# Streaming-encoder layer: projection weights split a block at a time ahead, and head pages prepared two score tiles ahead

## The chip, the cores and the metric

The kernel runs on one core of one Trainium2 chip. The metric is the device time of one execution in microseconds; less is better. It is given as the median of several runs.

A core has five engines that work side by side: TensorE (PE) multiplies matrices, VectorE (DVE), ScalarE (ACT) and GpSimd (POOL) work element by element, and SyncE (SP) issues the transfers (DMA). Each engine executes its own queue in order. An instruction that waits holds up all that stands behind it in the same queue.

## The reference, cut to what matters

One layer on a sequence of 1024 tokens of width 1024, in float32. The part that the change touches is the mixer:

```
h    = modulate(rmsnorm(x), shift, scale)
proj = h @ w_in                    # one input projection, its columns split:
  q_lat (256), kv_lat (128), k_rope (32)      -> latent attention, 8 heads
  ca_qkv (3 x 8 heads x 64)                   -> chunked attention, 8 heads
chunked: q, k normed per head; scores over a band of 9 chunks of 64 keys
         + a clipped relative bias; softmax; values
latent:  q, k, v from the normed latents by two up-projections; q, k normed,
         rotary on 32 of 96 dims; chunk-causal scores; softmax; values
x = x + gate * (concat(latent, chunked) @ w_out)
```

After it comes a gated MLP with a depthwise convolution, which the change does not touch.

## The kernel before, in words

**Numbers.** A float32 product is made of three matmuls on rounded parts: each operand is split into a high part (a copy, line 77, on ACT) and a low part (the difference, line 84, mostly on POOL), and `gemm3` (lines 150 to 157) multiplies high by high, high by low and low by high. So every block of weights has to be fetched, copied and subtracted before PE can use it.

**Fetching weights.** `load_w` (lines 175 to 196) takes a weight of the input projection in eight blocks of 128 rows. For each block it issues a DMA into a raw buffer (tag `wr`, 3 buffers), makes the high part on ACT and the low part on POOL (tag `ws`, 16 buffers). A block of up to 256 columns takes one `ws` buffer, a block of the 416-column weight `w_m` takes two, in two pieces each of its own raw buffer. For the second value weight a Square per block on ACT sums up the squares as well (line 192).

**Two kinds of work share the engines.** The first is attention: 32 units, first 16 of chunked attention, `(c, pair of heads p, half of the queries g, head o)`, then 16 of latent attention, `(m, group, head, half g)`. Each unit has four score tiles of 128 queries. A unit first needs its *pages*: `ca_pages` (713 to 732, for both heads of a pair at once) and `qk_page` (700 to 711) transpose the normed q and k on PE into one PSUM bank (tag `T`, a single buffer; the tiles are `q_ps`, `k_ps`, `mq_ps`, `mk_ps`) and split them on ACT, DVE and POOL. `Unit.scores` (742 to 834) multiplies into one of two score buffers (tag `S`), takes the minimum of the negated scores on DVE (`mc`, `mm`, lines 786 and 790), the exp on ACT (797), splits the probabilities into two halves of 16 bits on POOL and DVE (73 and 819) and transposes them by DMA (831). `Unit.values` (836 to 874) multiplies them by the values.

The second kind is called *fillers* (lines 931 and 932), in this order: `v0`, `qk1`, `qk2`, `v1`, `qk3` (the input projection, a pair of heads or two at a time), `m` (its latent columns, with transposes `lt_ps` of the normed latents into the bank `T`), `up0`, `up1` (the up-projections), `oca` (half of the output projection). Each is a generator; one step is six matmuls or so. A q/k or v projection has 32 steps: four output tiles of two rows of eight blocks, two blocks a step. `f_qk`, `f_v` and `f_m` call `load_w` for all eight blocks at their first step. In `f_qk` the ACT instructions of this call are queued behind `anchor["act"]`, the Square that was traced last in `qk_norm`.

**What sets the order.** The program is written once as a trace. The loop in lines 984 to 996 goes over the score tiles, prepares a unit just before its first tile (`need(u.need)`, `u.prep()`), traces its scores and, three tiles later, its values, and after each calls `pace` (968 to 975), which traces filler steps until their estimated cost makes up 1.9 times (chunked) or 0.5 times (latent) that of the piece of attention. `need` traces all steps of the fillers that a unit depends on. A scheduler then puts each engine's instructions into a queue: by their place in the trace, scores moved ahead by an offset of 400, probabilities and values by 200, and as inputs and buffers come free in its own estimate of time. On the chip the queues run as they were written. A filler's matmuls are also kept behind the score or value matmuls that were traced five pieces earlier (`trail`, `LAG`, lines 161 to 172), so that fillers cannot run far ahead of attention. A side stream `f_ada` on SP, DVE and PE computes further modulation vectors; `fill_step` (937 to 957) advances it with the fillers, and the rotary tables with `qk1`.

Behind these stages come the rest of the output projection and the MLP, lines 1004 onward.

Of the kernel before, what the change touches and what calls it, by code (L numbers as in the profile page):

```python
# [13 lines left out]
F32 = mybir.dt.float32  # L14
# [10 lines left out]
P = 128  # L25
# [3 lines left out]
ND = D // P  # L29
# [7 lines left out]
NM = QR + KVR + ROPE  # L37
# [27 lines left out]
def layer_kernel(ctx, tc, I, out):  # L65
# [49 lines left out]
    anchor = {}  # L115
# [56 lines left out]
            yield 3 * len(part) * max(107, w / 2.4 + 2.5)  # L172


    def load_w(name, src, ncol, he="a", ssw=None):
        tiles = []
        for k in range(ND):
            if ncol <= 256:
                w = hw.tile([P, 2, 256], F32R, name=f"{name}s{k}", tag="ws", bufs=16)
                hi, lo = w[:, 0, :ncol], w[:, 1, :ncol]  # L180
            else:
                wh = hw.tile([P, 512], F32R, name=f"{name}h{k}", tag="ws", bufs=16)
                wl = hw.tile([P, 512], F32R, name=f"{name}l{k}", tag="ws", bufs=16)
                hi, lo = wh[:, :ncol], wl[:, :ncol]
            for c0 in range(0, ncol, 256):
                c = slice(c0, min(c0 + 256, ncol))
                raw = hw.tile([P, 256], F32, name=f"{name}r{k}_{c0}", tag="wr", bufs=3)
                rw = raw[:, :c.stop - c0]
                anchor["sp"] = sp.dma_start(rw, src[:, k, c]).ins
                if ssw is not None:  # L190
                    junk = qtile(f"{name}j{k}")
                    act.activation(junk[:, :c.stop - c0], rw, AF.Square, accum_out=ssw[:, k:k + 1])
                hi_of(he, hi[:, c], rw)
                lo_of("p", lo[:, c], rw, hi[:, c])
            tiles.append((hi, lo))
        return tiles


    sp.dma_start(pos_i[:], I["pos"])
# [47 lines left out]
    wv0, wv0r = [], []  # L247
# [113 lines left out]

    qns, vts = {}, {}

    def f_qk(p):
        with tc.issue_after(anchor["act"]), tc.issue_after(r_last):
            w = load_w(f"wq{p}_", I["w_qk"][p], 256)
        for h in range(2):
            qns[p, h] = pgtile([P, 4, 256], F32, f"qn{p}_{h}")
        for t in range(0, NT, 2):
            pt = ps.tile([P, 512], F32, name=f"ipq{p}_{t}", tag="mm", bufs=2)  # L370
            yield from proj2(pt, t, w, 256)
            qk_norm(pt[:], f"{p}_{t}", qns[p, t // 4], t % 4)

    def f_v(pp):
        ssw = cst.tile([P, ND], F32, name=f"ssw{pp}") if pp else ssw0
        w = load_w(f"wv{pp}_", I["w_v"][pp], 256, ssw=ssw) if pp else wv0
        for t in range(0, NT, 2):
            h, j = divmod(t, 4)
            if t == 0:
                for i in range(2):  # L380
                    vts[2 * pp + i] = apg.tile([P, NT, 2, 2, 64], F16, name=f"v{2 * pp + i}", tag="v16", bufs=3)
            pt = ps.tile([P, 512], F32, name=f"ipv{pp}_{t}", tag="mm", bufs=2)
            yield from proj2(pt, t, w, 256)
            if t == 0:
                vscale["c", pp] = pow2_scale(f"c{pp}", ssw[:], hb[:], ND, 2.0 * D)
                sc = vscale["c", pp][0]
            for i in range(2):
                vt = vts[2 * pp + i][:, t:t + 2]
                src = pt[:].rearrange("p (t q a b) -> p t q a b", t=2, q=2, a=2)[:, :, i]
                act.activation(vt[:, :, :, 0, :], src, AF.Copy, scale=sc)  # L390
                dve.scalar_tensor_tensor(vt[:, :, :, 1, :], src, sc, vt[:, :, :, 0, :], op0=MUL, op1=SUB)
# [78 lines left out]
    def f_m():  # L470
        for _ in rope[0]:
            pass
        w = load_w("wm_", I["w_m"], NM)
        lat = {}
        for t in range(NT):
            h, j = divmod(t, 4)
            sl = slice(j * P, (j + 1) * P)
            pt = ps.tile([P, 512], F32, name=f"mp_{t}", tag="mm", bufs=2)
            yield from gemm3_f(pt[:, :NM], [(hT[k, h][:, 0, sl], hT[k, h][:, 1, sl]) + w[k] for k in range(ND)])
            raw = rtile(f"lat_{t}")  # L480
            act.activation(raw[:, :NM], pt[:, :NM], AF.Copy)
            sq = qtile(f"msq_{t}")
            ss = cst.tile([P, 2], F32, name=f"mss_{t}", tag="ss", bufs=4)
            r = cst.tile([P, 2], F32, name=f"mr_{t}", tag="rr", bufs=4)
            act.activation(sq[:, :QR], raw[:, :QR], AF.Square, accum_out=ss[:, 0:1])
            act.activation(sq[:, QR:QR + KVR], raw[:, QR:QR + KVR], AF.Square, accum_out=ss[:, 1:2])
            act.activation(sq[:, QR + KVR:NM], raw[:, QR + KVR:NM], AF.Square, accum_out=ssr[:, t:t + 1])
            pool.tensor_scalar(ss[:, 0:1], ss[:, 0:1], 1.0 / QR, EPS, op0=MUL, op1=ADD)
            rsqrt_mean(r[:], ss[:], KVR, cols=slice(1, 2))
            pool.tensor_scalar(raw[:, :QR], raw[:, :QR], r[:, 0:1], 1.0, op0=MUL, op1=MUL)  # L490
            pool.tensor_scalar(raw[:, QR:QR + KVR], raw[:, QR:QR + KVR], r[:, 1:2], 1.0, op0=MUL, op1=MUL)
            rope_apply(kr[:, t:t + 1, :], raw[:, QR + KVR:NM].unsqueeze(1), tabk, t, 1, raw[:, NM:NM + 64])
            lat[t] = raw
            if j == 3:
                for b in range(3):
                    ptt = ps.tile([P, 512], F32, name=f"lt_ps{h}_{b}", tag="T", bufs=TB)
                    for jj in range(4):
                        pe.transpose(ptt[:, jj * P:(jj + 1) * P], lat[4 * h + jj][:, b * P:(b + 1) * P], ident[:])
                    pg = pgtile([P, 2, 512], F32R, f"latT{h}_{b}")
                    gain = pk[:, C_GQL + b:C_GQL + b + 1]  # L500
                    act.activation(pg[:, 0], ptt[:], AF.Copy, scale=gain)
                    dve.scalar_tensor_tensor(pg[:, 1], ptt[:], gain, f32(pg[:, 0]), op0=MUL, op1=SUB)
                    latT[b, h] = pg
                    yield 436
# [410 lines left out]
    def mla_unit(gr, hh, g):  # L915
        o = hh % 2

        def prep():
            q = qk_page(lambda j: mq[gr, (4 * g + j) // 2][:, j % 2, hh, :], f"mq{gr}{hh}_{g}", QK, "Q", 2, None)
            k = qk_page(lambda j: mk[gr, (4 * g + j) // 2][:, j % 2, hh, :], f"mk{gr}{hh}_{g}", QK, "K", 3, gk_m[:QK])  # L920
            pages[gr, hh, g] = (q, k)
        u = Unit(f"m{gr}{hh}", 0, QK,
                 lambda: (pages[gr, hh, g][0], [pages[gr, hh, i][1] for i in range(g + 1)]),
                 lambda j: mv[gr, j // 2][:, j % 2, hh].rearrange("p a b -> p (a b)"),
                 g, False, None, o, oT_d[2 * gr + hh // 2], ("m", gr))
        u.prep = prep
        u.need = [f"up{gr}"] if g == 0 else ["up1"]
        u.needv = []
        return u
# [3 lines left out]
    done = set()  # L933
    side = [f_ada()]
    nside = [0]

    def fill_step():
        while fillers:
            key, gen = fillers[0]
            try:  # L940
                c = next(gen)
            except StopIteration:
                done.add(key)
                fillers.pop(0)
                continue
            if key == "qk1":
                if rope[0] is None:
                    rope[0] = rope_tables()
                with tc.issue_after(anchor["dve"]):
                    next(rope[0], None)  # L950
            if key not in ("v0", "up0", "up1", "oca"):
                nside[0] += c
                while nside[0] > 1700:
                    nside[0] -= 1700
                    next(side[0], None)
            return c
        return None
# [22 lines left out]
    first = [anchor["pe"]]  # L980
    units = [ca_unit(p, g, o) for p in range(4) for g in range(2) for o in range(2)]
    units += [mla_unit(gr, hh, g) for gr in range(2) for hh in range(4) for g in range(2)]
    tiles = [(u, i) for u in units for i in range(4 * u.g, 4 * u.g + 4)]
    for n in range(len(tiles) + DEPTH):
        if n < len(tiles):
            u, i = tiles[n]
            if i % 4 == 0:
                need(u.need)
                u.prep()
            pace(u.scores(i), R_CA if u.band else R_MLA)  # L990
        if n >= DEPTH:
            u, i = tiles[n - DEPTH]
            if i % 4 == 1:
                need(u.needv)
            if i % 2:
                pace(u.values(i), R_CA if u.band else R_MLA)
# [609 lines left out]
```

## Time and profile before

| | us |
|---|---|
| median of 3 runs | 1346.02 (1341.62 to 1346.54) |
| the profiled execution | 1345.89 |
| its span, first to last instruction | 1344.1 |
| PE busy | 1223.8 (91%) |
| DVE busy | 1096.2 (82%) |
| ACT busy | 622.7 (46%) |
| POOL busy | 578.1 (43%) |
| from the first score tile to the last value tile | about 86 to 627 |

In the profile's rows an instruction stands as `line engine operation out<-in`, by the names of the program's tiles with their numbers left out: `wq_s` and `wv_s` are split weights, `ipq`, `ipv` and `mp` the projections' results, `sc` and `sm` scores of chunked and latent attention, `pvc` and `pvm` values. `xN` is the count; then come the busy time in us and the mean duration of one in ns, and behind the second bar the time that the engine stood idle just before them and what ended it. In a timeline the start and the duration come first. In the views by stretch each engine has its busy time and count. A busy PE is not a PE at its peak: the granted clock says how fast it ran.

### The profile page before, as it was taken

To read this page: it belongs to the slowest core of one execution; us is meant where nothing else is said; L and a number is where in the kernel's file an instruction comes from. 1 tells how busy PE (TensorE), PEld (TensorE's weight loads), DVE (VectorE), ACT (ScalarE), POOL (GpSimd) and SP (SyncE) were. 2 spreads that over 40 slices of the span, in tenths; PEclk is the share of its full clock that TensorE was granted. 3 is DMA by queue.
4 is the path that set the end of the run, shared out by engine and by line. 5 is a ranking of instruction groups with operands and counts; after the bars stand their busy time and mean duration, and the time that the engine had idled before them with its cause. 6 is when DMAs were issued, how large, how long until landed. Compare 5 with 4: busy or idle time off the path is not lost.

```text
span 1344.1 us, 18696 instructions
## 1 busy us (share of the span) xinstructions
PE 1223.8 (91%) x6168; PEld 1003.8 (75%) x6168; DVE 1096.2 (82%) x1928; ACT 622.7 (46%) x1132; POOL 578.1 (43%) x610
## 2 busy tenths in 40 slices
PE   4899798998877798886998999999999998999998
PEld 3788587896655567765776888888888886888886
DVE  6978798864679987894989988988899997687667
ACT  4453546443555544563376444444434444433431
POOL 5464557565646763354634444444445431000000
PEclk9899798998787889996999999999999998999999
DMA  8415577854413477779911333333323326943441
GB/s 323 138 35 116 135 177 179 192 127 110 87 32 80 94 153 165 141 150 252 377 49 47 126 110 133 103 122 98 133 102 118 126 98 241 390 141 117 130 161 63
DMA packets 223689, 190.57 MB, mean 142 GB/s; under 512 B 148708, under 2 KB 166884, under 8 KB 223592
## 3 DMA queue, kind: packets, MB, share of 16 engines
q1 hardware_dynamic: 223592, 189.38, 49.1%
q8 instruction: 48, 0.79, 0.2%
q14 instruction: 49, 0.40, 0.1%
HBM read 117.24 MB, written 37.49 MB: 115 GB/s over the span
## 4 chain that ended last, share of the span: by engine, by line
PE 41%; DVE 10%; issue 3%; ACT 2%; DMA 1%; POOL 1%; SPq 0%; DVEq 0%; ACTq 0%; POOLq 0%
PE p L1082 7%; PE p L1084 7%; PE p L1083 7%; PE dnA_P L1417 2%; PE dnA_P L1419 2%; PE dnA_P L1418 2%; PE dnB_P L1419 1%; PE dnB_P L1418 1%; PE dnB_P L1417 1%; DVE u L1253 1%; DVE u L1254 1%; PE op L154 1%; PE dnA L1417 1%; PE dnA L1419 1%; PE dnA L1418 1%
## 5 line engine op out<-in xcount | busy, mean ns | idle before, releaser
L77 ACT ACTIVATE dnP<-dnr 128x1024 fp32r<-128x1024 f32 x73 | 77.5, 1064 | 117.5 <-PE dnA_P L1419 46.4
L1391 DVE TENSOR_TENSOR dnP<-dnr,dnP 128x1024 fp32r<-128x1024 f32 x72 | 87.9, 1223 | 52.6 <-ACT dnP L77 52.6
L73 POOL TENSOR_SCALAR hlm<-Pm,rim 128x512 f16<-128x512 f32 (+3 forms) x96 | 68.8, 726 | 83.5 <-DVE rim L800 22.3
L84 POOL TENSOR_TENSOR wf<-wu,wf 128x512 fp32r<-128x512 f32 x22 | 38.8, 1762 | 116.3 <-ACT wf L77 116.3
L1253 DVE SCALAR_TENSOR_TENSOR u<-c,cvp,u 128x1023 f32<-128x1023 f32 x44 | 64.8, 1513 | 27.8 <-ACT u L1252 27.8
L73 POOL TENSOR_SCALAR hlc<-Pc,ric 128x640 f16<-128x640 f32 (+2 forms) x64 | 50.8, 797 | 61.0 <-ACT Pc L797 20.8
L819 DVE SCALAR_TENSOR_TENSOR hlm<-Pm,rim,hlm 128x512 f16<-128x512 f32 (+3 forms) x96 | 68.0, 719 | 9.8 <-POOL hlm L73 9.7
L797 ACT ACTIVATE Pc<-sc,mc 128x640 f32<-128x640 f32 (+2 forms) x64 | 42.1, 658 | 53.1 <-DVE mc L786 35.9
L797 ACT ACTIVATE Pm<-sm,mm 128x128 f32<-128x128 f32 (+3 forms) x64 | 47.1, 736 | 41.7 <-DVE mm L790 24.2
L84 POOL TENSOR_TENSOR wb<-wu,wb 128x512 fp32r<-128x512 f32 x22 | 38.1, 1732 | 64.5 <-ACT wb L77 50.7
L1252 ACT ACTIVATE u<-c,cvp 128x1024 f32<-128x1024 f32 x44 | 52.3, 1237 | 27.8 <-DVE c L1351 19.2
L1254 DVE SCALAR_TENSOR_TENSOR u<-c,cvp,u 128x1022 f32<-128x1022 f32 x44 | 63.8, 1488 | 0.0
L859 PE MATMUL pvm<-PTm,vt 128*128 128x256 f16 (+1 forms) x320 | 45.7, 294 | 17.0 <-DMA PTm<-hlm 9.9
L819 DVE SCALAR_TENSOR_TENSOR hlc<-Pc,ric,hlc 128x640 f16<-128x640 f32 (+2 forms) x64 | 51.6, 809 | 9.3 <-POOL hlc L73 8.7
L155 PE MATMUL ipq<-wq_s,hT 128*128 128x256 f32 x192 | 56.0, 292 | 0.1
L859 PEld LDWEIGHTS <-vt 128*128 128x128 f16 x320 | 31.6, 109 | 32.7 <-DMA PTm<-hlm 15.0
L154 PE MATMUL ipq<-wq_s,hT 128*128 128x256 f32 x192 | 55.8, 293 | 0.0
L156 PE MATMUL ipq<-wq_s,hT 128*128 128x256 f32 x192 | 55.4, 289 | 0.0
L77 ACT ACTIVATE wc<-ws 128x512 fp32r<-128x512 f32 x21 | 13.3, 632 | 88.0 <-DVE ws L1101 82.2
L1418 PE MATMUL dnA_P<-dnP 128*128 128x512 f32 x132 | 51.4, 389 | 0.0
L1419 PE MATMUL dnA_P<-dnP 128*128 128x512 f32 x132 | 51.3, 389 | 0.0
L1417 PE MATMUL dnA_P<-dnP 128*128 128x512 f32 x132 | 51.2, 389 | 0.0
(442 smaller groups left out, 4428.4 us busy)
## 6 DMA issues: line engine op xcount, KB each, us to landing
wu<-w_up SPq DMA_DIRECT2D x44, 512.0 KB, 3.5
dnr<-g_d SPq DMA_DIRECT2D x73, 256.0 KB, 2.8
aw<-w_ada SPq DMA_DIRECT2D x48, 256.0 KB, 3.5
g_d<-u SPq DMA_DIRECT2D x22, 512.0 KB, 3.0
dnr<-w_down SPq DMA_DIRECT2D x44, 256.0 KB, 5.3
adaw<-w_ada_a SPq DMA_DIRECT2D x16, 512.0 KB, 6.3
x<-x SPq DMA_DIRECT2D x16, 512.0 KB, 9.0
g_d<-gs SPq DMA_DIRECT2D x22, 256.0 KB, 2.8
```

What stands on the lines that cost most here:

```text
L73: pool.tensor_scalar(o, i, s, 1.0, op0=MUL, op1=MUL)
L77: act.activation(o, i, AF.Copy)
L797: act.activation(pr[:, :n], sv, AF.Exp, bias=m[:], scale=-1.0, accum_out=rsum[:, 0:1])
L819: dve.scalar_tensor_tensor(hl[:, w:2 * w], pp, ri[:], hl[:, :w], op0=MUL, op1=SUB)
L1082: pe.matmul(pt, sh, pg[:, 0], start=(k == 0 and not add), stop=False, skip_group_check=skip)
L1083: pe.matmul(pt, sh, pg[:, 1], start=False, stop=False, skip_group_check=skip)
L1084: last = pe.matmul(pt, sl, pg[:, 0], start=False, stop=(k == 3), skip_group_check=skip)
L1253: dve.scalar_tensor_tensor(u[:, 1:], c[:, :S - 1], cvp[:, cv + 1:cv + 2], u[:, 1:], op0=MUL, op1=ADD)
L1391: r = f(*a, **k)
L1417: pe.matmul(pt, sh, w[:, 0, 0], start=start, stop=False, skip_group_check=add)
L1418: pe.matmul(pt, sh, w[:, 1, 0], start=False, stop=False, skip_group_check=add)
L1419: pe.matmul(pt, sl, w[:, 0, 0], start=False, stop=stop, skip_group_check=add)
```

## The change

It has two parts, made together.

*Weights a block at a time.* `load_w` becomes a generator, `load_steps`, that yields after each block. `coming` makes one generator for each of the weights to come, `one_ahead` takes one block from it, and `weights` takes what is left. While the fillers `qk1`, `qk2`, `v1` and `qk3` run, every third step takes one block of the next filler's weights: all eight for a q/k or v weight, at most four for `w_m`. Each time the block's ACT instructions are queued behind the `qk_norm` Square that was traced last; that holds for `v1` and `m` now as well, which had no such order before. `qk1`'s own weights are fetched at its first step as before.

*Pages two tiles ahead.* At the third tile of each unit the loop looks at the unit of the tile two places on, which is the next unit's first. If all that it needs is done, its `prep` is traced there, ahead of that third tile's scores, and left out later. If not, it is prepared as before.

```diff
-    def load_w(name, src, ncol, he="a", ssw=None):
+    def load_w(*a, **k):
         tiles = []
+        for _ in load_steps(tiles, *a, **k):
+            pass
+        return tiles
+
+    def load_steps(tiles, name, src, ncol, he="a", ssw=None):
         for k in range(ND):
...
             tiles.append((hi, lo))
-        return tiles
+            yield
...
+    ahead = {}
+
+    def coming(key):
+        if key not in ahead:
+            tiles, ssw = [], None
+            if key == "m":
+                g = load_steps(tiles, "wm_", I["w_m"], NM)
+            elif key[0] == "q":
+                g = load_steps(tiles, f"wq{key[2]}_", I["w_qk"][int(key[2])], 256)
+            else:
+                ssw = cst.tile([P, ND], F32, name=f"ssw{key[1]}")
+                g = load_steps(tiles, f"wv{key[1]}_", I["w_v"][int(key[1])], 256, ssw=ssw)
+            ahead[key] = g, tiles, ssw
+        return ahead[key]
+
+    def one_ahead(key):
+        g, tiles, _ = coming(key)
+        if len(tiles) < (4 if key == "m" else ND):
+            with tc.issue_after(anchor["act"]):
+                next(g)
+
+    def weights(key):
+        g, tiles, ssw = coming(key)
+        with tc.issue_after(anchor["act"]):
+            for _ in g:
+                pass
+        return tiles, ssw
+
     def f_qk(p):
-        with tc.issue_after(anchor["act"]), tc.issue_after(r_last):
-            w = load_w(f"wq{p}_", I["w_qk"][p], 256)
+        with tc.issue_after(r_last):
+            w, _ = weights(f"qk{p}")
...
     def f_v(pp):
-        ssw = cst.tile([P, ND], F32, name=f"ssw{pp}") if pp else ssw0
-        w = load_w(f"wv{pp}_", I["w_v"][pp], 256, ssw=ssw) if pp else wv0
+        w, ssw = weights(f"v{pp}") if pp else (wv0, ssw0)
...
-        w = load_w("wm_", I["w_m"], NM)
+        w, _ = weights("m")
...
+    nstep = [0]
...
+            if key in ("qk1", "qk2", "v1", "qk3"):
+                nstep[0] += 1
+                if nstep[0] % 3 == 0:
+                    one_ahead(fillers[1][0])
...
+    ready = []
     tiles = [(u, i) for u in units for i in range(4 * u.g, 4 * u.g + 4)]
     for n in range(len(tiles) + DEPTH):
         if n < len(tiles):
             u, i = tiles[n]
-            if i % 4 == 0:
+            if i % 4 == 0 and u not in ready:
                 need(u.need)
                 u.prep()
+            if i % 4 == 2 and n + 2 < len(tiles):
+                v = tiles[n + 2][0]
+                if all(k in done for k in v.need):
+                    ready.append(v)
+                    v.prep()
             pace(u.scores(i), R_CA if u.band else R_MLA)
```

## The prediction, made before the result was known

> **What bounds the kernel now.** I read the busy time by stretch first, then the projections' matmuls, the waits of PE, and the timeline around the two longest stops. The stretches below are cut where the work changes; the columns are PE, PEld, DVE, ACT and POOL busy (with instruction counts), granted TensorE clock, DMA share, GB/s.
>
> ```profile
> 100.00:135.00 35.00, 35.00 (x265) 31.38 (x266) 28.39 (x91) 12.24 (x26) 15.21 (x16) 1.00 0.51 118
> 135.00:150.00 15.00, 9.20 (x40) 5.57 (x39) 14.59 (x43) 7.64 (x17) 5.93 (x7) 0.77 0.62 144
> 150.00:170.00 20.00, 16.16 (x84) 12.46 (x85) 11.93 (x37) 11.59 (x24) 13.62 (x18) 0.74 0.58 129
> 170.00:199.00 29.00, 28.78 (x210) 25.15 (x210) 26.86 (x70) 13.35 (x31) 17.14 (x19) 1.00 0.71 170
> 199.00:216.00 17.00, 13.05 (x62) 9.58 (x60) 15.55 (x37) 12.09 (x35) 12.82 (x14) 0.70 0.76 196
> 216.00:283.00 67.00, 67.00 (x519) 60.45 (x519) 55.38 (x156) 31.19 (x76) 40.21 (x48) 1.00 0.83 189
> 283.00:316.00 33.00, 32.58 (x180) 28.29 (x178) 20.44 (x59) 16.91 (x58) 24.99 (x53) 1.00 0.39 100
> 316.00:340.00 24.00, 16.68 (x77) 13.73 (x76) 8.37 (x16) 6.85 (x17) 6.03 (x15) 0.76 0.32 77
> 398.00:435.00 37.00, 26.80 (x116) 21.06 (x115) 33.74 (x104) 22.34 (x54) 23.24 (x23) 0.72 0.30 76
> 435.00:487.00 52.00, 38.44 (x196) 28.96 (x195) 50.02 (x145) 27.59 (x64) 38.18 (x37) 0.80 0.54 109
> 487.00:612.00 125.00, 113.48 (x648) 89.94 (x647) 104.11 (x263) 66.39 (x141) 58.22 (x75) 0.99 0.75 157
> ```
>
> Between 100 and 283 us PE is full wherever the clock is 1.00; only 135 to 170 and 199 to 216 have holes, with the clock down too. From 398 to 487 DVE is the full engine (33.74 of 37, 50.02 of 52), so nothing that only feeds PE helps there. What starves PE in the two holes shows in the projections' own matmuls, PE first in each row (`ipq` of the q/k weights in the first two rows, `ipv` of the v weights in the last):
>
> ```profile
> 135.00:150.00 15.00, 1.22 (x8) 0.80 (x7) 0.59 (x1) 0.77 0.62 144
> 150.00:167.00 17.00, 6.88 (x36) 5.66 (x36) 0.00 (x0) 0.70 0.58 128
> ...
> 199.00:216.00 17.00, 3.77 (x14) 2.51 (x12) 0.00 (x0) 0.00 (x0) 0.70 0.76 196
> ```
>
> No more than 44 and 14 of the 192 matmuls of a projection run in the holes. The POOL timeline says why: the low halves of the next weights are made there, one by one, long after the projection could have begun.
>
> ```profile
> 149.23 2.13 POOL L84 TENSOR_TENSOR wq_s<-wq_r,wq_s 128x256 fp32r<-128x256 f32 x3 [5.67 <-ACT wq_s L77]
> ...
> 166.71 0.72 POOL L84 TENSOR_TENSOR wq_s<-wq_r,wq_s 128x256 fp32r<-128x256 f32 x1
> ```
> ```profile
> 213.24 1.15 POOL L84 TENSOR_TENSOR wv_s<-wv_r,wv_s 128x256 fp32r<-128x256 f32 x1
> ```
>
> Each output tile needs all eight blocks, so qk2 cannot flow before 167.4 nor v1 before 214.4.
>
> **The change, part by part.** *Weights.* Counting the filler steps, a q/k or v projection has 32; one block every third step brings all eight in by step 24, so qk2, v1 and qk3 start with their weights split. Eight ACT operations (for v1 eight Squares more) and eight POOL operations per set move; none is added. They leave two places where ACT and POOL had them in a burst and go to stretches like 100 to 135, where POOL is busy 15.21 of 35 and ACT 12.24: hidden there. If that cover were gone, 8 x 0.73 = 5.8 us of POOL per set would be back, which is about today. The eight DMAs of a set move with them on SP, where each waits for one of three raw buffers with the transposes of the probabilities queued behind:
>
> ```profile
> SPq L189 <- POOL wv_s L84: 3.3, 2, 2.4
> ```
>
> That is 3.3 us in two waits for v1, whose blocks came in a burst; spread out they should wait less. I take nothing, and at worst the same again for each of three sets, 9.9, which only delays transposes, not PE's own weights.
>
> What PE lost in the holes: idle (15 - 9.20) + (20 - 16.16) + (17 - 13.05) = 13.6 us; through the clock 9.20 x 0.23 + 16.16 x 0.26 + 13.05 x 0.30 = 10.2 us. Together 23.8 us, the upper end. DVE is late next: between 135 and 283 it has 14.59 + 11.93 + 26.86 + 15.55 + 55.38 = 124.3 us of work, and the densest stretch beside a full PE, 170 to 199, runs it at 26.86/29 = 0.926. At that density 124.3 takes 134.2 us in place of 148: **-13.8 us**, which I take. The lower end is the first hole's 5.8 us of idle alone. The gain is passed on: m, up0 and up1 follow the projections in one list, and the stretches behind are ruled by their own engines.
>
> ```profile
> PE sc L765 <- ACT Pc L797: 7.4, 5, 2.2
> PE ipv L154 <- DVE mc L786: 3.1, 1, 3.1
> ```
>
> The clock term is the doubtful one. In these waits (PE, 100 to 283; total, times, longest) no idle time exceeds 3.1 us, and yet the clock fell to 0.77, 0.74 and 0.70. The Trainium skill (TensorE: Matmul & The Clock Gate, Part 1: The HAM clock gate) says that the half clock comes after at least one idle window of about 3.4 us; the trace does not agree, several shorter stops did it. By that rule no clock would return with the idle time, and the upper end would be 13.6 in place of 23.8.
>
> *The last half of m.* The m weights may go only four blocks ahead; the other four are now traced behind the last Square of qk3. Before, they waited for buffers alone.
>
> ```profile
> L84 POOL TENSOR_TENSOR wm_l<-wm_r,wm_h 128x256 fp32r<-128x256 f32 (+1 forms) x10 | 7.6, 780 | 1.4 <-ACT wm_h L77 1.4
> ```
>
> Eight pieces on POOL take 8 x 0.78 = 6.2 us; PE has the first four blocks to work on, 12 matmuls 0.19 us apart (the two starts of `mp` in the next fence), 2.3 us. Queued behind the wait on ACT are the exps of (c,3,0,0), whose pages PE can meanwhile transpose. Between 0 and 6.2 - 2.3 = 3.9; I take the middle, **+2**.
>
> *Pages.* By the costs in the pace loop, the next unit's `need` is met two tiles ahead for all but (c,1,0,0), (m,0,0,0) and (m,0,0,1). The place where it tells is (c,3,1,0):
>
> ```profile
> 330.94 0.35 PE L155 MATMUL mp<-wm_l,hT 128*128 128x416 f32 x1
> 331.13 0.35 PE L156 MATMUL mp<-wm_h,hT 128*128 128x416 f32 x1
> 331.32 0.60 PE L697 MATMUL q_ps<-ident,qn 128*128 128x128 f32 x4
> 333.33 0.67 PE L765 MATMUL sc<-k,qh 128*128 128x512 f32 x2 [1.42 <-POOL qh L725]
> 334.76 0.65 PE L697 MATMUL k_ps<-ident,qn 128*128 128x128 f32 x4 [0.75 <-DVE ql L724]
> 336.96 0.48 PE L765 MATMUL sc<-k,qh 128*128 128x128 f32 x1 [1.55 <-DVE k L730]
> ```
>
> PE stands 1.42 + 0.75 + 1.55 = 3.7 us for a page that was traced behind the latent transposes, which share its one PSUM bank. Two tiles earlier it comes ahead of them: **-3.7**. At most it gives the stretch's whole loss, 7.3 idle + 16.68 x 0.24 = 11.3; at worst the latent transposes now wait for the page, +3.7. For the latent heads the waits of PE from 398 to 612 are these:
>
> ```profile
> PE mq_ps L697 <- DVE qn L468: 5.8, 3, 2.4
> ...
> PE mk_ps L697 <- DVE mq_0l L706: 2.0, 1, 2.0
> PE mk_ps L697 <- DVE rim L800: 1.4, 1, 1.4
> PE mq_ps L697 <- DVE rim L800: 1.2, 1, 1.2
> ```
>
> The first belongs to the two units that are not prepared ahead. The rest is 4.6 us, the most that 14 early units can win. Against it stands what they overtake:
>
> ```profile
> L709 ACT ACTIVATE mk<-mk_ps,gk_m 96x512 fp32r<-96x512 f32 x15 | 10.2, 681 | 10.0 <-PE mk_ps L697 9.4 <-PE sm L771 0.5
> ...
> L705 ACT ACTIVATE mq_1h<-mq_ps 96x512 fp32r<-96x512 f32 x8 | 4.7, 591 | 7.5 <-PE mq_ps L697 7.5
> ```
> ```profile
> L710 DVE SCALAR_TENSOR_TENSOR mk<-mk_ps,gk_m,mk 96x512 fp32r<-96x512 f32 x16 | 11.6, 724 | 2.2 <-ACT mk L709 2.1
> ...
> L706 DVE TENSOR_TENSOR mq_1l<-mq_ps,mq_1h 96x512 fp32r<-96x512 f32 x8 | 5.4, 673 | 0.2
> ```
>
> Per unit 0.72 + 0.67 = 1.4 us of DVE and 0.68 + 0.59 = 1.3 us of ACT go in front of the running unit's minimum and exp: 0 to 14 x 1.4 = 19.6, or 37.4 with ACT, if every one delayed a tile. They ran among these tiles before as well, so I take **0** for both together.
>
> Sum: -13.8 + 2 - 3.7 + 0 = -15.5. The profiled execution took 1345.89 us (span 1344.1 and 1.8 around it), 0.1 under the median of 1346.02, so the forecast is **1330 us**.
>
> **The rivals.**
> *Pages overtake (slower).* In the latent stage the early page steps stand in front of the minimum that frees a score buffer. For it: DVE is at 50.02 of 52. Against it: PE has 113.48 of 125 later on, with DVE at 104.11, so some delays are covered. Half-way between 19.6 and 37.4, 28.5 us: 1346 - 15.5 + 28.5 = 1359. It turns the result from 15.5/14 = 1.1 us a unit on.
> *DVE keeps the pace (no change).* The fillers may run at most some three tiles ahead of the attention (the LAG rule); if DVE, 14.59 of 15 in the first hole, holds the attention, the fillers stop again. Then the 5.8 us remains, less 2: 1342.
> *The change does not do what it says.* The raw weights already came early; only the split was late, and the ACT queue could put it late again, behind exps that wait for DVE. Then only the page part is left, -3.7 + 2: 1344. I count it with the one before.
> *All comes back.* The whole 23.8, and 7.5 at the page (half-way between 3.7 and 11.3), less the 2: 1346 - 29.3 = 1317. By that clock rule of the Trainium skill (TensorE: Matmul & The Clock Gate, Part 1) it would come back by 10.2 less, 1327.
>
> **How the numbers follow.** About 0.5% (6.7 us) is what a measurement of this kernel can tell from no change. Chances: forecast 0.53 (1323 to 1339), all comes back 0.12, DVE keeps the pace or no effect 0.18, pages overtake 0.17. So faster 0.65, within 0.5% 0.18, slower 0.17. The range reaches from 1317, with half of the second case below it, to 1357, with rather more than half of the last above it: 15 in 100 left out. The likeliest case alone is 1323 to 1339.
>
> **What would show it.** Right: the low halves of the second q/k set are made before 135 us, `ipq` and `ipv` matmuls have no hole, the clock stays near 1.00 to the end of the projections, and m begins near 269 in place of 283; then no PE wait at the page of (c,3,1,0). Wrong: the holes stay with all weights split (DVE), m opens with a stop on its own low halves, or the stretch from the first up-projection to the last attention tile (366 to 612) grows by over 5 us, with more ACT waits on `mm`. A gain that is there at 283 and gone at 612 would break the step that says it is passed on.

## The result, and the profile after

The kernel after takes **1333.17 us** (median of 4 runs, 1329.0 to 1334.63), the kernel before beside it 1344.99 (4 runs, 1341.62 to 1346.54). The ratio is **0.9915**, 95% interval 0.9891 to 0.9939: 0.85% faster. The profiled execution after took 1334.5 us (span 1332.7 and 1.8 around it), 11.4 less than the one before.

First the two signs of the split. In the rows of the timeline (start, us, engine, line, operation), the low halves of the second q/k set on POOL, the last six of eight, after the change:

```profile
113.42 2.13 POOL L84 TENSOR_TENSOR wq_s<-wq_r,wq_s 128x256 fp32r<-128x256 f32 x3 [1.33 <-PE sc L797]
121.53 1.47 POOL L84 TENSOR_TENSOR wq_s<-wq_r,wq_s 128x256 fp32r<-128x256 f32 x2
123.68 1.39 POOL L84 TENSOR_TENSOR wq_s<-wq_r,wq_s 128x256 fp32r<-128x256 f32 x1
```

All are made before 125.1 us, where the first of them stood at 149.23 before. And busy time by stretch after the change, cut where the same work now lies (us; PE, PEld, DVE, ACT, POOL busy with counts; granted TensorE clock; DMA share; GB/s):

```profile
102.00:137.00 35.00, 35.00 (x266) 31.32 (x266) 33.06 (x104) 15.43 (x35) 23.25 (x24) 1.00 0.71 165
137.00:150.00 13.00, 11.12 (x87) 9.88 (x87) 10.34 (x32) 9.93 (x22) 6.79 (x10) 1.00 0.58 131
150.00:184.00 34.00, 33.42 (x240) 28.49 (x239) 32.09 (x88) 21.90 (x56) 25.61 (x30) 1.00 0.66 150
184.00:226.00 42.00, 38.49 (x280) 33.42 (x279) 37.32 (x102) 21.30 (x51) 21.80 (x27) 0.96 0.84 179
226.00:264.00 38.00, 38.00 (x287) 33.31 (x287) 32.78 (x87) 14.47 (x34) 22.27 (x25) 1.00 0.78 170
264.00:298.00 34.00, 28.35 (x149) 22.64 (x147) 27.02 (x71) 18.27 (x54) 22.47 (x41) 0.90 0.58 134
```

Both holes are all but gone: no stretch of this cut up to 264 has a clock under 0.96, where before it stood at 0.77, 0.74 and 0.70 in three stretches. What is left shows in a finer cut: from 190 to 200 us PE is busy 7.71 us, with a clock of 0.83. The page of (c,3,1,0), in the timeline of PE, comes early and nobody waits for it:

```profile
284.26 1.11 PE L729 MATMUL q_ps<-ident,qn 128*128 128x128 f32 x4
...
289.63 0.66 PE L729 MATMUL k_ps<-ident,qn 128*128 128x128 f32 x4
...
297.96 0.45 PE L797 MATMUL sc<-k,qh 128*128 128x512 f32 x2
```

The scores of (c,3,1,0) start at 297.96 in place of 333.33, without a bracket for a wait. From first and last matmuls by name the shift of each stage can be followed:

| mark in the PE timeline | before | after | shift |
|---|---|---|---|
| end of `qk2` | 196.81 | 183.81 | -13.0 |
| end of `v1` | 248.76 | 226.51 | -22.2 |
| first `mp` (m starts) | 282.88 | 264.14 | -18.7 |
| end of `up0` | 398.25 | 374.88 | **-23.4** |
| last `sm` (end of latent scores) | 611.63 | 595.67 | **-16.0** |
| first MLP matmul `p` | 712.11 | 699.34 | -12.8 |
| span | 1344.1 | 1332.7 | -11.4 |

So 23.4 us are won up to the end of `up0`. Of those, 7.4 go again among the latent heads, 3.2 in the output projection's stage and 1.4 behind it. From 102 us to the end of `up0` both kernels do the same work, so one window each, before first and then after, says what the 23.4 us were:

```profile
102.00:398.25 296.25, 265.00 (x1624) 223.00 (x1623) 221.80 (x630) 143.36 (x362) 168.72 (x236) 0.89 0.56 130
```
```profile
102.00:374.88 272.88, 246.98 (x1628) 210.58 (x1627) 224.71 (x633) 142.20 (x363) 166.69 (x235) 0.96 0.62 138
```

PE's idle time falls from 31.25 to 25.90, by 5.4 us. PE's busy time falls by 18.0 at the same number of matmuls, as the clock rises from 0.89 to 0.96 (265.00 x 0.89 = 236 and 246.98 x 0.96 = 237). Three quarters of the gain is clock.

### The profile page after: what moved, and what is told of

Read it like the earlier page. It is cut to its first block, busy times and chain, and to the rows that moved or that the text cites. A ratio compares the mean times of both kernels' runs of the same rounds, so it can differ in the third digit from the quotient of the medians.

```text
span 1332.7 us, 18710 instructions
## 1 busy us (share of the span) xinstructions
PE 1212.8 (91%) x6168; PEld 997.1 (75%) x6168; DVE 1088.7 (82%) x1928; ACT 622.3 (47%) x1132; POOL 572.3 (43%) x610
## 4 chain that ended last, share of the span: by engine, by line
PE 48%; DVE 3%; DMA 2%; issue 1%; ACT 1%; POOL 0%; SPq 0%; POOLq 0%; DVEq 0%
PE p L1125 10%; PE p L1126 10%; PE p L1127 10%; PE dnA_P L1460 2%; PE dnA_P L1461 2%; PE dnA_P L1462 2%; PE dnB_P L1461 1%; PE dnB_P L1460 1%; PE dnB_P L1462 1%; PE dnA L1461 1%; PE dnA L1460 1%; PE dnA L1462 1%; PE dnB L1461 1%; PE dnB L1462 1%; PE dnB L1460 1%
## 5 line engine op out<-in xcount | busy, mean ns | idle before, releaser
L73 POOL TENSOR_SCALAR hlm<-Pm,rim 128x512 f16<-128x512 f32 (+2 forms) x96 | 65.4, 691 | 77.5 <-DVE rim L832 32.0
L1296 DVE SCALAR_TENSOR_TENSOR u<-c,cvp,u 128x1023 f32<-128x1023 f32 x44 | 58.6, 1372 | 27.8 <-ACT u L1295 27.8
L84 POOL TENSOR_TENSOR wb<-wu,wb 128x512 fp32r<-128x512 f32 x22 | 42.2, 1920 | 75.0 <-ACT wb L77 59.6
L73 POOL TENSOR_SCALAR hlc<-Pc,ric 128x640 f16<-128x640 f32 (+2 forms) x64 | 48.0, 753 | 54.5 <-DVE ric L832 25.8
L851 DVE SCALAR_TENSOR_TENSOR hlm<-Pm,rim,hlm 128x512 f16<-128x512 f32 (+2 forms) x96 | 65.9, 696 | 5.5 <-POOL hlm L73 5.2
```

The source lines that it names most:

```text
L73: pool.tensor_scalar(o, i, s, 1.0, op0=MUL, op1=MUL)
L84: (pool if eng == "p" else dve).tensor_tensor(o, i, f32(hi), op=SUB)
L851: dve.scalar_tensor_tensor(hl[:, w:2 * w], pp, ri[:], hl[:, :w], op0=MUL, op1=SUB)
```

## The experiments

Twelve kernels ran, each in five rounds beside the kernel before on the same chip. "up0" is the end of `up0`, "latent" the time from there to the last latent score tile, both in the one profiled execution; they place a loss, and the ratio decides. A single execution can lie several us off the median of its kernel: the profiled one of the weights alone took 1344.39 us (median 1339.43), that of the last row 1323.16 (median 1326.19), and the first one of the kernel before 1345.89, where its later medians are 1341.0 to 1342.7.

| run | ratio | interval | up0 | latent |
|---|---|---|---|---|
| before, first profile | | | 398.25 | 213.4 |
| before once more | 0.9991 | 0.9974 to 1.0007 | 399.40 | 211.1 |
| weights alone | 0.9975 | 0.9960 to 0.9991 | 394.24 | 215.1 |
| pages alone | 1.0010 | 0.9997 to 1.0024 | 389.92 | 218.5 |
| weights, chunked pages | 0.9938 | 0.9919 to 0.9956 | 376.90 | 222.3 |
| weights, latent pages | 1.0007 | 0.9994 to 1.0021 | 392.89 | 215.1 |
| weights, page of (c,3,1,0) | 0.9964 | 0.9950 to 0.9979 | 386.96 | 217.3 |
| all but that page | 1.0012 | 0.9994 to 1.0029 | 388.70 | 218.8 |
| the change, m not anchored | 0.9961 | 0.9942 to 0.9980 | 380.15 | 222.8 |
| weights, chunked pages, latent queues of before | **0.9872** | 0.9851 to 0.9893 | 377.50 | 214.8 |
| before, latent queues of weights and chunked pages | 1.0076 | 1.0054 to 1.0098 | 395.24 | 220.7 |
| chunked pages, latent queues of before | 0.9979 | 0.9967 to 0.9992 | 391.76 | 212.2 |
| weights, page of (c,3,1,0), latent queues of before | **0.9880** | 0.9860 to 0.9900 | 379.85 | 209.4 |

### Which part brings it

The theories of the first four runs: A, the weights bring the gain, and latent pages ahead give some back; B, what is given back goes with the early start of the latent heads and not with their pages; C, the chunked pages speed up the projections themselves.

The weights alone (the lines of the pages go):

```diff
-            if i % 4 == 2 and n + 2 < len(tiles):
-                v = tiles[n + 2][0]
-                if all(k in done for k in v.need):
-                    ready.append(v)
-                    v.prep()
```

> Weights split ahead, every page prepared at its unit's first tile as before. Theory A (the weights carry the gain, the early pages of the latent heads give some 8 us of it back): m begins near 265 us as with both parts, the stretch from the end of up1 to the last latent score is near 145 us as before and not 153, and the time is near 1345 - 16 = 1329. Theory B (the give-back has nothing to do with the pages; the latent stage takes longer whenever the projections end earlier): m near 265, the latent stretch near 153, the time 1337 or more, since the page of (c,3,1,0) is late again. Theory C (the early pages of the chunked heads are what speeds up the projections, by giving DVE its work earlier): m begins only near 275 and the time is near 1340.

Measured: 1339.43 us, 0.9975. The pages alone (weights loaded as in the kernel before, the five lines above kept):

> Pages two tiles ahead, weights fetched all at a filler's first step as before. Theory A: the holes of PE near 135 to 170 and 199 to 216 stay, m begins near 283, the stop at the page of (c,3,1,0) is gone for 4 us, and the latent stage gives 8 us back: near 1349. Theory B: no give-back, since the projections end as before: near 1341. Theory C: m begins near 274, the time is near 1337.

Measured: 1343.91 us, 1.0010. The weights with the pages of the chunked heads, and with those of the latent heads:

```diff
-                if all(k in done for k in v.need):
+                if v.band and all(k in done for k in v.need):
```

> Both parts, but pages ahead for the chunked heads alone; the latent ones at their first tile as before. Theory A: all up to the end of up1 as with both parts (24 us ahead of before), the latent stretch 145 us in place of 153, the time near 1326. Theory B: the latent stretch 153 as with both, the time 1334.

Measured: 1335.66 us, 0.9938.

```diff
-                if all(k in done for k in v.need):
+                if not v.band and all(k in done for k in v.need):
```

> Both parts, but pages ahead for the latent heads alone; the chunked ones at their first tile as before. Theory A: the stop at the page of (c,3,1,0) is back, and with it about 4 us more than with both parts, 1337; the latent stretch 153. Theory B: 1337 too, with the latent stretch as with both. Theory C: m begins near 275 and the time is near 1343.

Measured: 1344.29 us, 1.0007.

Neither part alone reaches the 0.5% that the prediction called measurable; together they do. With the weights alone m does start at 269.89, 13.0 us early, and most of that gain is then lost in m's own stage: m ends 4.5 us early and `up0` 4.0. The profile shows two reasons. The scheduler put the projections' matmuls ahead of attention, so the scores of (c,2,1,*) end at 277.20, 8.2 us *later* than before (269.01): part of the early start was only an exchange of order. How large a part, a count of matmuls tells. At m's start PE had done about as many since 102 us as the kernel before had at 278.70, so some 8.8 of the 13.0 us are work done earlier (kernel before, then weights alone):

```profile
102.00:278.70 176.70, 162.89 (x1128) 138.68 (x1128) 150.29 (x423) 86.48 (x200) 100.71 (x115) 0.92 0.69 162
```
```profile
102.00:269.89 167.89, 156.62 (x1131) 137.26 (x1130) 144.36 (x398) 82.96 (x194) 98.03 (x112) 0.95 0.66 152
```

The second reason is that the page of (c,3,1,0) still stands behind the latent transposes, as the timeline of PE shows for the weights alone:

```profile
320.51 0.60 PE L530 MATMUL lt_ps<-ident,lat 128*128 128x128 f32 x4
322.68 0.66 PE L530 MATMUL lt_ps<-ident,lat 128*128 128x128 f32 x4 [1.56 <-DVE latT L534]
...
327.54 0.60 PE L729 MATMUL q_ps<-ident,qn 128*128 128x128 f32 x4
329.56 0.67 PE L797 MATMUL sc<-k,qh 128*128 128x512 f32 x2 [1.42 <-POOL qh L757]
330.98 0.63 PE L729 MATMUL k_ps<-ident,qn 128*128 128x128 f32 x4 [0.75 <-DVE ql L756]
333.16 0.33 PE L797 MATMUL sc<-k,qh 128*128 128x128 f32 x1 [1.55 <-DVE k L762]
```

These are the same 1.42, 0.75 and 1.55 us of waiting as in the kernel before. The scores start only 3.8 us early, while the projections were done 13.0 early.

The holes did not close with the weights alone either, though PE waits for no split weight there any more. PE's idle time from 102 us to m's start is 13.8 us before, 11.3 with the weights alone, 14.7 with the pages alone, 7.4 with the weights and the chunked pages and 6.0 after the change. With the weights alone PE now waits for transposed probabilities and for the exp, and around these waits DVE is full (waits of PE, 102 to 269.89, then two stretches; DVE is the third column of times):

```profile
PE pvc L891 <- DMA PTc<-hlc: 6.7, 3, 3.3
PE sc L797 <- ACT Pc L829: 3.5, 2, 2.8
```
```profile
128.00:141.00 13.00, 9.72 (x73) 8.35 (x73) 12.75 (x36) 3.99 (x8) 9.18 (x9) 0.94 0.86 214
200.00:212.00 12.00, 6.01 (x37) 4.41 (x37) 11.62 (x34) 4.60 (x10) 2.49 (x4) 0.82 0.59 132
```

A falls: without latent pages ahead the latent stretch is as long (222.3) as with them (220.8 after the change), and its forecasts for the weights alone (1329 us) and for this run (1326) are missed by 10 each. B's figure for it came (1334 forecast, 1335.66 measured), but B does not say why an early start should cost, and the queues below show that it need not. C is right in direction: adding the chunked pages brings m's start from 269.89 to 266.08 and takes a third off the idle time that was left, though with the weights alone m began at 269.89 and not only at 275 (the time that C gave for it, 1340 us, did come).

### The one page

```diff
-                if all(k in done for k in v.need):
+                if (v.nm, v.g) == ("c30", 1) and all(k in done for k in v.need):
```

> The weights part, and of the pages ahead only that of (c,3,1,0). Theory C1 (that page opens the m stage: with the weights early, it is the one thing that holds m, the latent transposes and up0 back): m starts 13 us before the kernel before, the scores of (c,3,1,0) 30 us or more before, up0 ends 17 to 21 us before, and the time is about that of the weights with all chunked pages, ratio 0.994 (0.992 to 0.996). Rival C2 (the early pages of (c,1,1,0), (c,2,0,0), (c,2,1,0) and (c,3,0,0) bring it, by giving DVE work earlier all along the projections): up0 ends only 4 to 8 us before, ratio 0.997 as with the weights alone.

Measured: 1337.06 us, 0.9964; `up0` ends 11.3 us early. And the reverse, with `!=` in place of `==`:

> Both parts, but the page of (c,3,1,0) is built where it was. C1: m starts 14 to 19 us before the kernel before, but the gain goes in the m stage: the scores of (c,3,1,0) come 4 to 8 us before and up0 ends 4 to 8 us before; ratio 0.997 to 1.000, as for the weights alone or with the latent pages. C2: nearly the whole change, up0 ends 15 us before or more, ratio 0.992 to 0.994.

Measured: 1343.54 us, 1.0012; the scores of (c,3,1,0) come 9.2 us early and `up0` ends 9.6 early. C1's figures are missed by little (9.2 and 9.6 in place of 4 to 8 us, 1.0012 in place of at most 1.000), C2's by far. As it ran, everything else together without this page is worth nothing; the latent stretch had grown as well (218.8), and this kernel was not run with the order of before held, as others are below. The first run, with the page, fell between the two theories; the queues below say why.

### The last blocks of m

```diff
-        w, _ = weights("m")
+        w, _ = weights("m", False)
```

With `False`, `weights` traces the rest without `issue_after(anchor["act"])`.

> The change, with the last four blocks of the m weights not traced behind the last Square of qk3. By the step of the prediction (2 us lost there): 2 us under the change, ratio 0.990. Rival (after the change PE waits 0.4 us for those blocks, so there is nothing to win): within 0.5 us of the change, ratio 0.991 to 0.992; m's stage, from its first to its last matmul, is as long as with the change, 72 us.

Measured: 1336.90 us, 0.9961; m's stage took 76.6 us, with the change 72.1. Nothing is won, and the rival's equal time did not come either: of the 4.5 us more in m's stage, 3.6 are PE's busy time for the same 359 matmuls (69.04 against 65.47, clock 0.89 against 0.95). In the change PE's wait for these blocks is one of 0.4 us (waits of PE, 264 to 348, after the change):

```profile
PE mp L154 <- ACT wm_h L77: 0.4, 1, 0.4
```

### Where the gain went behind `up0`

First the scatter of a single profile:

> The kernel before once more, to see how far two profiled executions of the same instructions lie apart, stage by stage. Theory D1 (the give-back of some 8 us behind the projections is the change's): from the end of up0 to the last score tile the two agree within 1.5 us (213.4 us in the first profile), and so do the ends. Rival D2 (a good part of it is the scatter of single executions): that stretch differs by 3 us or more. The ratio of the times is 1.000 within 0.0015.

Measured: 1340.97 us, 0.9991. At the marks the two profiles of the kernel before lie up to 2.4 us apart, the latent stretch 2.3, the span 2.2. That lies between D1's bound and D2's. The latent stretch of the change and its relatives is 7 to 9 us longer than in the first profile; two profiles are few to call that no scatter, and the ratios below settle it.

What differs there is not the code. The scheduler that puts each engine's queue in order goes by its own estimate of when inputs come free, and with another beginning it estimates another state at the latent heads. With the weights alone its queues from `up0` on are those of the kernel before, and that stretch is 215.1. With the chunked pages ahead they differ, on PE by some 290 of 1079 instructions that stand in another place, though this part of the trace is unchanged. The head of PE's queue at `up1`, kernel before and then weights with chunked pages (tiles and number of matmuls):

```
vspm 1, qu 6, ku 1, pvm 4, ku 2, mq 1, qu 6, sm 4, mk 4, ku 3, qu 6, sm 8, mq 4, ku 3, sm 6, mk 4, pvm 8
vspm 1, qu 6, ku 1, pvm 4, ku 2, mq 1, qu 6, sm 4, ku 3, qu 6, mk 4, ku 3, sm 8, mq 4, pvm 4, sm 6, pvm 4
```

The k page of the next head (`mk`) stands nine matmuls later. To test the order by itself, it was written down: each engine's instructions from the first latent unit on, by their place in the trace, and each tied behind the one ahead of it.

```diff
+QUEUES = {"PE": [(72, 12), (108, 12), (0, 15), (61, 1), (15, 9), (62, 1),
+...
+    traced = list(tc.nc.cur_bb.bb.instructions)
+    for eng, runs in QUEUES.items():
+        row = [i for i in traced[k0:] if i.engine == getattr(mybir.EngineType, eng)]
+        queue = [row[s + j] for s, c in runs for j in range(c)]
+        for x, y in zip(queue, queue[1:]):
+            tc.add_manual_dep(y, x.name, mybir.DependencyInfo(
+                mybir.DependencyClass.NoSync, mybir.DependencyReason.DATA), reason="queue")
```

The kernel of the weights and chunked pages, with the order of the kernel before:

> The weights part and the chunked pages ahead, as in the run of that name, but from the first latent unit's pages to the end of attention each engine's instructions stand in the order in which the scheduler had put them in the kernel before (1079 on PE, 574 on DVE, 222 on ACT, 146 on POOL, 147 on SP, each tied behind the one ahead of it). Theory E1 (the give-back behind up0 is the scheduler's other queue there, since its own estimate of time starts from another state): up0 ends 21 us before the kernel before; from there to the last score tile 211 to 215 us, as in the two profiles of before (213.4 and 211.1), in place of 222; the end comes 17 to 20 us before; ratio 0.986 (0.984 to 0.988). Rival E2 (something that does not come earlier holds the latent heads, transfers or POOL, or DVE is the bound there): the stretch stays at 219 to 223 us and the ratio at 0.994 (0.992 to 0.996).

Measured: **1324.85 us**, 0.9872. The kernel before, with the order of the other:

> The other way round: the kernel before, with the queues from the first latent unit's pages on that the scheduler made for the weights with the chunked pages. E1: up0 ends where it did in the kernel before, within 2 us; from there to the last score tile 219 to 223 us in place of 213; ratio 1.006 (1.004 to 1.008). E2: the stretch is 211 to 215 us, ratio 1.000 within 0.0015.

Measured: 1353.10 us, 1.0076. The same instructions in two orders, each way round: one order costs some 9 to 11 us more than the other (0.9938 against 0.9872, 1.0076 against 0.9991), and the intervals lie apart. E1 holds, but for `up0` in the second kernel, which ended 3.0 us early in place of at most 2; E2 falls. The kernel before, tied in its own order, was not run; but the two tied kernels moved in opposite directions by like amounts, so the tie itself is not what moved them. The latent stretch by windows, in the order before, after, weights and chunked pages with the old order, before with the new order:

```profile
398.25:611.63 213.38, 178.47 (x955) 139.76 (x954) 187.25 (x507) 115.79 (x256) 119.64 (x135) 0.90 0.62 131
```
```profile
374.88:595.67 220.79, 182.28 (x954) 142.59 (x954) 186.04 (x507) 115.45 (x256) 112.57 (x135) 0.89 0.62 127
```
```profile
377.50:592.34 214.84, 178.59 (x955) 140.19 (x954) 186.01 (x509) 116.43 (x257) 119.38 (x135) 0.90 0.63 131
```
```profile
395.24:615.96 220.72, 179.32 (x956) 139.28 (x956) 186.51 (x507) 115.60 (x256) 115.35 (x134) 0.90 0.62 128
```

The work is the same, no engine is busier by more than 4 us, and the transfers' share does not move. The waits of PE in these stretches (total, times, longest) for the same four:

```profile
PE sm L771 <- ACT Pm L797: 9.7, 11, 1.9
PE pvm L859 <- DMA PTm<-hlm: 6.5, 7, 1.8
```
```profile
PE sm L803 <- ACT Pm L829: 16.3, 15, 2.3
PE pvm L891 <- DMA PTm<-hlm: 11.4, 8, 3.3
```
```profile
PE sm L906 <- ACT Pm L932: 10.9, 12, 1.9
PE pvm L994 <- DMA PTm<-hlm: 9.0, 8, 2.6
```
```profile
PE sm L872 <- ACT Pm L898: 13.6, 14, 2.0
PE pvm L960 <- DMA PTm<-hlm: 11.9, 7, 2.7
```

With the new order PE reaches a score tile before its buffer is read out by the exp, and values before their transposed probabilities have landed: 28 us of these two waits after the change, 16 before. Which of the moved instructions does it was not tried. Nor was the change itself run with the old order: its trace has the latent pages two tiles earlier, so that order does not fit it. For it the cause is taken over from its relative with the chunked pages alone, whose latent stretch is as long.

### The parts again, with the order held

> The chunked pages ahead without the weights part, and with the queues of the kernel before from the first latent unit's pages on, so that what is won up to the end of up0 is kept. Theory F1 (the two parts bring more together than each for itself): up0 ends 8 us before the kernel before, as in the run of the pages alone, the end too; ratio 0.994 (0.992 to 0.996), so that weights alone (0.9975) and this come to 0.9915 and both together to 0.987. Rival F2 (with the queues held fixed the parts add up): 0.987 - 0.9975 + 1 = 0.990 (0.988 to 0.9915), up0's end 14 us before.

Measured: 1338.78 us, 0.9979.

> The weights part and the page of (c,3,1,0) alone, with the queues of the kernel before from the first latent unit's pages on. F1 and E1: up0's end 11 us before the kernel before, kept to the end, ratio 0.992 (0.990 to 0.994): more than half of what both parts bring, but the other four chunked pages are needed for the rest. Rival (the one page is the whole of the pages' part): 0.987 (0.985 to 0.989), up0's end 20 us before.

Measured: 1326.19 us, **0.9880**.

With the latent queues of the kernel before, which the weights alone have by themselves, the weights bring 0.25%, the chunked pages 0.21% and both 1.28%: more than twice the sum. F1's direction holds, its 0.994 for the pages was too much. The second expectation fails: its rival is right. The weights and this single page bring all that can be measured; the other chunked pages ahead make the difference between 0.9880 and 0.9872, which is none, though PE's idle time from 102 us to m's start is 6.9 us with them and 11.7 without (the two kernels with the order held). There are five of them: (c,0,1,0) counts too, whose k page is transposed at 103.97 us with them and at 110.13 without. In its first run (0.9964) the one page was hidden by the scheduler's order, which put the first latent scores (381.13) ahead of the end of `up0` (386.96). With the order held the one page moves the end of `up0` from 394.24 (weights alone) to 379.85.

Both these kernels, 0.9872 and 0.9880, are faster than the kernel before, and by their medians than the change (0.9915); the interval of the change overlaps a little with each of theirs.

## Why the prediction was right, and where its steps were not

The forecast of 1330 us, faster, is near the 1333.17 measured, yet two of its terms were wrong and cancelled in part. By the ratios the weights alone are worth 3.4 us, 10.4 less than taken, and the page behind them 12.8, 9.1 more; that the sum came near is luck to this extent.

- **Weights, -13.8.** The size at m's start came out, -13.0 with the weights alone, but only some 8.8 of it is work done earlier. The step that failed is "The gain is passed on: m, up0 and up1 follow the projections in one list". Alone, 4.0 us of 13.0 are left at the end of `up0` and 0.25% (3.4 us) in the time; at the last latent score (611.63 to 609.30) 2.3, which is the sign that the prediction had named for this step. The early m start was partly bought with later attention, and the next thing late was the page. The prediction treated the two as separate terms of a sum. The rival that DVE keeps the pace came half true: the split was early, and yet 11.3 of 13.8 us of idle time stayed with the weights alone, with DVE busy 12.75 of 13 and 11.62 of 12 us around the waits. It is the chunked pages, which the prediction did not count on here, that brought the idle time down to 7.4.
- **Pages, -3.7 at (c,3,1,0).** The place and the mechanism, a page behind the latent transposes in one bank, were right; the term was mis-sized. Without the weights part the chunked pages are worth 2.8 us (0.9979, order held), near the 3.7. With the weights early and the order held, the one page is worth 14.4 us at the end of `up0` (394.24 to 379.85, in single profiles) and 0.95% of the time (0.9975 to 0.9880, 12.8 us, some 3 either way): clearly over the 3.7, and about at the upper bound of 11.3 or over it. Term and bound came from the stretch as it was, with the projections late; once they are early, most of what they won waits for this page.
- **Latent pages, 0.** The pages themselves: with and without them 0.9915 and 0.9938, with overlapping intervals, so no more can be said. The rival that pages overtake did not come: the longer latent stretch is there without them. But the prediction missed that the scheduler would write the latent queues anew; in the profile of the change the latent stretch is 7.4 us longer. It named the sign: the stretch behind `up0`'s start, 366 to 612, grew by only 2.2 us there (348.04 to 595.67, 247.6 against 245.4), since `up0` itself had become 5.2 shorter and hid most of the loss. The sign was cut at the wrong place.
- **The last half of m, +2.** Nil: one wait of 0.4 us, and taking the anchor away won nothing.
- **SP and DMA, nothing.** No PE wait between 102 and 264 is for a split weight after the change, though the raw blocks do stand longer: between 100 and 264 SP waits 7.2 us on the split of q/k blocks, which had 0.6 before, while the v1 blocks fell from 3.3 to 0.8:

```profile
SPq L194 <- POOL wq_s L84: 7.2, 6, 3.2
```

- **Idle and clock.** The upper end of 23.8 us, which the rival of all coming back used, was reached up to `up0` (23.4), if not by the sum named: 18.0 of it is clock and 5.4 idle, where the prediction had 10.2 and 13.6. By the rule of the Trainium skill (TensorE: Matmul & The Clock Gate, Part 1: The HAM clock gate) that puts the half clock after at least one idle window of about 3.4 us, no clock could have come back, as no wait here exceeded 3.1 us before. The rows of the equal work do not agree with it.

Sum of the profile: -23.4 + 7.4 + 3.2 + 1.4 = -11.4. That an order of the queues makes such a loss as the 7.4 is shown for the weights with the chunked pages; for the change itself it is inferred. For the 3.2 us in the output projection's stage no cause was found: from the last latent score to the MLP's first matmul the kernels took 98.2 to 104.7 us (two profiles of before: 100.5 and 99.7), in no order that goes with a part of the change, so it stays open and may be scatter.

## What to carry to other kernels

Where a scheduler fills the queues, a change at the start can rewrite the order far behind it: compare the order of the unchanged stages as well, and if it moved, hold the old one fixed to learn what the change itself is worth. Two stops in a row on one path are not two terms of a sum: taking away the first lets the second grow by what was won, so the second is bounded by its old wait and the first gain together. An early start of the next stage counts only if no other work was pushed back for it; a window over equal work, with the same number of matmuls, tells the two apart. And a hole that closes for one supplier can stay for the next: look at what the engine waits for after the change, not only at whether the old wait is gone.

## What the runs showed of the hardware

In these profiles the loss of short stops showed more in the clock than in idle time. Up to the end of `up0` the kernel before had waits of at most 3.1 us and was granted 0.89; after the change the longest wait was 1.9 us (of `pvc` on a transposed probability, five such waits with 4.5 us in all) and the clock 0.96:

```profile
PE pvc L891 <- DMA PTc<-hlc: 4.5, 5, 1.9
```

For the same 1624 and 1628 matmuls PE was busy 265.0 and 247.0 us. In the latent stretch 32 to 42 us of idle time in 209 to 223 went with a clock of 0.87 to 0.91 in all fourteen profiles, whatever the order. Idle time alone does not set the clock: the weights alone had 32.8 us of it there at 0.87, the kernel before 34.9 at 0.90.
